# Compressing the samples' values before their keys, with the prompt's last weights kept, and a narrow weight unit laid out without holes

## The chip, the cores and the metric

The kernel runs on one core of one Trainium2 chip. The metric is the device time of one execution in microseconds. TensorE (PE) does the matrix products and has its own weight loads (PEld), VectorE (DVE), ScalarE (ACT) and GpSimd (POOL) work beside it, and SyncE (SP) issues nearly all of the transfers (DMA).

## The reference, cut to what matters

One layer of a hybrid decoder works on 512 prompt tokens and on 8 samples of 4 tokens (a model width of 1024, all in float32). A first feed-forward block (FFN1) is followed by a mixing stage, in which a state-space part and a sparse attention part share one input projection and one output projection, and then by a second feed-forward block (FFN2).

```python
def compress(k, w1, w2, pe):              # keys and values, each with weights of its own
    ch = k.reshape(bsz, n_str, CMP_STRIDE, NSA_KV_HEADS, HEAD_DIM)
    first = jnp.einsum('bnsgd,sdh->bngh', ch, w1[:CMP_STRIDE])
    second = jnp.einsum('bnsgd,sdh->bngh', ch, w1[CMP_STRIDE:])
    pre = first[:, :-1] + second[:, 1:] + jnp.einsum('sd,sdh->h', pe, w1)
    return jax.nn.gelu(pre) @ w2
...
    kc = compress(k_c, lw['cmp_k_w1'], lw['cmp_k_w2'], lw['cmp_k_pe'])
    vc = compress(v_c, lw['cmp_v_w1'], lw['cmp_v_w2'], lw['cmp_v_pe'])
```

`compress` is applied twice: to the prompt's own keys and values (512 tokens), and to the cached ones of the 8 samples (1024 tokens each, read through a page table). The order in which keys and values are compressed does not change what is computed.

## The kernel before, in words

**Products.** Every float32 operand of a large product is split into a high part and a remainder, and each block of 128 rows costs three matmuls: high by high (L319), remainder of the data by high weight (L320), high by remainder of the weight (L321). `gemm` at L312 issues them.

**Weights.** Weights come in units of 128 x 8 x 128 (512 KB), through the DMA queue of SP, into a pool of three buffers for each part (`w_hi` and `w_lo`), which are taken in turn. `Weights.get` (L174) hands out the next unit. Units that have a name were split ahead, during FFN1, by `Ahead.run` (L200), and lie in DRAM as `high_` and `rest_` arrays, so that getting one is two DMAs of 512 KB (L181). `c0` and `c1` are the two halves of the keys' compression weights, `c2` and `c3` those of the values'. `dg` is a narrow unit of 128 x 8 x 32, the weights of the gates; it lies in a 128 x 8 x 128 buffer with holes, so that each of its DMAs moves 1024 pieces of 128 bytes.

**Order.** The mixing stage is written as generators that a table interleaves. Its first phase projects (`q0`, `vw`, `kc`, `c0`, `dg`, ... in the table's order, where `c0` to `c3` there stand for prompt compression steps), the second runs attention of the prompt (steps `p`), compression of the samples (steps `k`) and more projections (`x`). The program's instructions are then ordered for each engine at build time, by a scheduler that simulates a timeline; so a small edit can move instructions of engines that it does not name.

**Compression of the prompt** (`compress_prompt`, L881): for kv = 0 (keys, `c0` and `c1`) and kv = 1 (values, `c2` and `c3`) 48 matmuls at L893, a transpose at L902, a GELU, a small product (L910 for keys, L923 for values). The keys end in `Kc`, whose remainder parts are put in place by four small DMAs (L920). `po` of L923, a tile named `tp`, reads `ge_a`, which lies in a pool that is closed at the end of the first phase; tiles of the next phase that take its place (`at_m`, `at_p`, and the pool `S.more`) wait until L923 has read it.

**Compression of the samples** (`compress_sample`, L1376): four times over, two samples' pages are loaded into `pg`; then for kv = 0 and kv = 1 the pages are split (`cs_H` on ACT at L1394; `cs_L` at L1395, the first sample's on DVE, the second's on POOL), multiplied in 48 matmuls (24 for each half unit), and finished by `cs_x` (L1402) and a GELU. In the first of the four rounds the units are got from DRAM once more: `c0` and `c1` for keys, `c2` and `c3` for values, the last of them into a buffer of `S.more`. The remainder `cs_L` of kv = 0 lies in the phase's pool `gp`, that of kv = 1 in `S.more`.

**Attention of the prompt** (`attend_prompt`, L1021): scores against the compressed keys (`sc<-Kc`, L1035), scores of a window (`sc<-K`, L1056 to L1058), their softmax (`at_m` on DVE L1065 and L1067, `at_p` on ACT L1066, then POOL L1069), transposes (L1097) and products with the values (L1087).

Of the kernel before, what the change touches and what calls it, by code (L numbers as in the profile page):

```python
# [25 lines left out]
F32 = mybir.dt.float32  # L26
# [3 lines left out]
AF = mybir.ActivationFunctionType  # L30
# [121 lines left out]
    IN_COL[f"x{_i}"] = 512 + 128 * _i  # L152


class Weights:


# [5 lines left out]

    def fetch(self, ap):

        _, nk, m = ap.shape
        raw = self.raws[0].tile([128, 8, 128], F32, name="w_raw", bufs=self.raws[1])
        self.dma.dma_start(raw[:, :nk, :m], ap)
        return raw

    def load(self):
# [2 lines left out]
    def get(self, pool=None):  # L174
        nc, ap = self.nc, self.units[self.n]
        hi, lo = ((pool or self.pool).tile([128, 8, 128], F32R, name=n, bufs=1 if pool else 3) for n in ("w_hi", "w_lo"))
        if isinstance(ap, str):
            self.n += 1
            _, nk, m = self.ahead.units[ap].shape
            for t, src in zip((hi, lo), self.ahead.parts[ap]):  # L180
                self.dma.dma_start(t.bitcast(F32)[:, :nk, :m], src[:, :nk, :m])  # L181
            return hi, lo
        if not self.raw:
            self.load()
        raw = self.raw.pop(0)
        self.n += 1
        _, nk, m = ap.shape
        nc.scalar.activation(hi[:, :nk, :m], raw[:, :nk, :m], AF.Copy)  # L188
        nc.vector.tensor_tensor(lo[:, :nk, :m], raw[:, :nk, :m], hi.bitcast(F32)[:, :nk, :m], op=OP.subtract)  # L189
        return hi, lo  # L190


class Ahead:
# [6 lines left out]
    def run(self, W, pool):  # L200
        nc, names = self.nc, list(self.units)
        raw = W.fetch(self.units[names[0]])
        yield
        for i, n in enumerate(names):
            _, nk, m = self.units[n].shape
            hi = pool.tile([128, 8, 128], F32R, name="a_hi", bufs=2)
            r, h = raw[:, :nk, :m], hi.bitcast(F32)[:, :nk, :m]
            nc.scalar.activation(hi[:, :nk, :m], r, AF.Copy)  # L208
            nc.vector.tensor_tensor(r, r, h, op=OP.subtract)  # L209
            for dst, t in zip(self.parts[n], (h, r)):  # L210
                W.dma.dma_start(dst[:, :nk, :m], t)
            if i + 1 < len(names):
                raw = W.fetch(self.units[names[i + 1]])
            yield
# [3 lines left out]
def step_kernel(ctx, tc, I, O, stop=99):  # L218
    nc = tc.nc
# [5 lines left out]
    def f32(t):  # L225
        return t.bitcast(F32)
# [5 lines left out]
    def split(hi, lo, src):  # L232
        nc.scalar.activation(hi, src, AF.Copy)  # L233
        nc.vector.tensor_tensor(lo, src, f32(hi), op=SUB)  # L234

    def pcol(k):
        a, b = P_OFF[k]
        return par[:, a:b]
# [13 lines left out]
    units = []  # L252
# [8 lines left out]
    seen = []  # L261
    named = {}

    def unit(name, ap):
        named[name] = ap
        units.append(name)

    for step in T0_ORDER + T1_ORDER + T2_ORDER:
        if step in ("c0", "c1", "c2", "c3"):
            unit(step, I["w1"][int(step[1])])  # L270
        elif step == "dg":
            unit(step, I["wdg"])
        elif step == "k" and seen.count("k") < 2:
            units.extend(f"c{seen.count('k') * 2 + i}" for i in range(2))
        elif step == "x":
            unit(f"x{seen.count('x')}", I["win"][IN_TILES.index(f"x{seen.count('x')}")])
        elif step in IN_TILES:
            unit(step, I["win"][IN_TILES.index(step)])
        seen.append(step)
# [8 lines left out]
    W = Weights(nc, wpool, units, nc.sync, ahead)  # L288
# [281 lines left out]
    def gelu2(x, pool, n):  # L570

        p = x.shape[0]
        a = pool.tile([128, n], F32, name="ge_a", bufs=1)
        nc.scalar.activation(a[:p], x, AF.Square)
        nc.vector.tensor_scalar(a[:p], a[:p], 0.044715, 1.0, op0=MUL, op1=ADD)
        nc.vector.tensor_tensor(a[:p], a[:p], x, op=MUL)
        nc.scalar.activation(a[:p], a[:p], AF.Tanh, scale=GELU_C)
        nc.vector.scalar_tensor_tensor(a[:p], a[:p], 1.0, x, op0=ADD, op1=MUL)
        return a
# [225 lines left out]
    def proj_kvq(n1, S, gp, pp):  # L805
# [6 lines left out]
        for kv in range(2):  # L812
            pe = pcol("pe")[:, kv * 16:kv * 16 + 16].rearrange("p (a s) -> p s a", a=2)
            nc.vector.tensor_copy(cT[kv][:, :, 64:66], pe)
        cmp_ = compress_prompt(S, cT, gp, pp)
        def tile_(name):
            t = IN_TILES.index(name)
# [63 lines left out]
    def compress_prompt(S, cT, gp, pp):  # L881
        w2 = pcol("w2")
        for kv in range(2):
            cH = gp.tile([128, 8, 66], F32R, name="cH")
            cL = gp.tile([128, 8, 66], F32R, name="cL")
            split(cH, cL, cT[kv])

            ps = pp.tile([128, 2, 128], F32, name="mm", bufs=2)
            for half in range(2):
                wh, wl = W.get()  # L890
                for k in range(8):
                    for x, w in ((cH, wh), (cL, wh), (cH, wl)):
                        nc.tensor.matmul(ps[:66, half], x[:, k], w[:, k], start=k == 0 and x is cH and w is wh,  # L893
                                         stop=k == 7 and w is wl)
                if half == 0:
                    yield
            fs = gp.tile([128, 8, 66], F32, name="cp_f", tag="cL").rearrange("p a b -> p (a b)")[:66, :256]
            nc.vector.tensor_copy(fs, ps[:66].rearrange("p a b -> p (a b)"))

            px = pp.tile([128, 512], F32, name="tp", bufs=2)  # L900
            for half in range(2):
                nc.tensor.matmul(px[:, :65], fs[:, half * 128:half * 128 + 128], ident[:66, half:half + 65],  # L902
                                 start=half == 0, stop=half == 1)
            nc.vector.tensor_copy(S.peb[:, kv:kv + 1], px[:, 64:65])
            x = gp.tile([128, 2, 32], F32, name="cp_x", bufs=1)
            nc.scalar.activation(x.rearrange("p g n -> p (g n)"), px[:, :64], AF.Identity, bias=S.peb[:, kv:kv + 1])
            ge = gelu2(x.rearrange("p g n -> p (g n)"), gp, 64)
            po = pp.tile([128, 512], F32, name="tp", bufs=2)
            if kv == 0:
                nc.tensor.matmul(po[0:64, :64], w2[:, 0:64], ge, start=True, stop=True)  # L910
                kc = gp.tile([128, 2, 32], F32, name="cp_kc", tag="cp_x", bufs=1).rearrange("p g n -> p (g n)")[:64]
                nc.scalar.activation(kc, po[0:64, :64], AF.Copy, scale=0.5)
                for g in range(2):
                    src = kc[:, g * 32:g * 32 + 32]
                    for dup in range(2):
                        nc.scalar.activation(S.Kc[dup * 64:dup * 64 + 64, g, 0], src, AF.Copy)
                    lo_ = gp.tile([64, 32], F32R, name="cp_lo", bufs=2)
                    nc.vector.tensor_tensor(lo_, src, f32(S.Kc)[0:64, g, 0], op=SUB)
                    for dup in range(2):
                        nc.sync.dma_start(f32(S.Kc)[dup * 64:dup * 64 + 64, g, 1], f32(lo_))  # L920
            else:
                for g in range(2):
                    nc.tensor.matmul(po[0:32, g * 64:g * 64 + 64], ge[:, g * 32:g * 32 + 32], w2[:, 64:128],  # L923
                                     start=True, stop=True)
                nc.scalar.activation(S.Vc, po[0:32, 0:128].rearrange("p (g d) -> p g d", g=2), AF.Copy, scale=0.5)
            yield
# [448 lines left out]

    def compress_sample(S, gp, pp):  # L1376
        w2 = pcol("w2")
        units = []
        for pr in range(4):
            raw = []  # L1380
            for b in range(2):
                raw.append(S.pages.tile([128, 8, 256], F32, name="pg", bufs=3))
                pages(raw[b], I["cmp"], pr * 2 + b)
            for kv in range(2):
                if pr == 0:
                    units.append([W.get(), W.get(pool=S.more if kv else None)])
                wts = units[kv]

                cH = gp.tile([128, 16, 16, 8], F32R, name="cs_H", bufs=2)
# [1 line left out]
                for b in range(2):  # L1391
                    o = (slice(None), slice(None), slice(b * 8, b * 8 + 8))
                    r = raw[b][:, :, kv * 128:kv * 128 + 128].rearrange("p i (a n) -> p a i n", n=8)
# [18 lines left out]
                dst = S.vcS[:, pr] if kv else S.kcT[:, pr * 2:pr * 2 + 2].rearrange("p b c -> p (b c)")  # L1412
# [283 lines left out]
```

## Time and profile before

| | us |
|---|---|
| median of three runs | 1272.11 |
| the three runs | 1269.2, 1272.11, 1685.08 |
| the profiled execution | 1272.05 |
| its span, from first to last instruction | 1270.3 |
| PE busy in the span | 1230.0 (97 %) |

The profiled execution is told by its span, and 1.75 us lie around it. Time stamps below are microseconds from the span's start. The mean granted clock of TensorE in the span was 0.987 of full speed. The run of 1685.08 was a disturbed one.

The mixing stage lies between 395 and 785 us; the first phase meets the second between 485 and 520 us.

### The profile page before, as it was taken

What the parts mean: (1) busy time and instruction counts of PE and PEld (TensorE: products, weight loads), DVE (VectorE), ACT (ScalarE), POOL (GpSimd) and SP (SyncE); (2) the same over time, 40 slices, a digit from 0 to 9 for tenths busy, and PEclk for the clock granted to TensorE, in tenths of its full rate; (3) what the DMA queues carried; (4) which work ended last, traced back from release to release, by engine and by line L of the source; (5) the groups of instructions that cost most, each with busy time, mean ns of one, the idle gap of its engine ahead of it and who ended that gap; (6) DMA issues with size and microseconds to landing.
All of it is one profiled execution on the core that took longest, in us unless ns stands there. A gap on an engine that the chain in (4) does not pass through costs nothing.

```text
span 1270.3 us, 24550 instructions
## 1 busy us (share of the span) xinstructions
PE 1230.0 (97%) x9810; PEld 1165.2 (92%) x9810; DVE 743.8 (59%) x1525; ACT 479.5 (38%) x913; POOL 242.3 (19%) x225
## 2 busy tenths in 40 slices
PE   7999999999999998999999999999999999999994
PEld 7999999999999997888877677899999999999994
DVE  5443443454543887766777675557666666644446
ACT  5343333443333444444544223334333333332223
POOL 0000000002232322542433543000000000035440
PEclk9999999999999998999999999899999999999997
DMA  8666665688773857443341581453222222223312
GB/s 315 201 229 207 235 216 213 226 292 273 257 237 113 261 208 260 134 137 133 105 134 35 172 322 39 160 199 96 86 84 84 86 95 86 80 76 92 92 46 71
DMA packets 89314, 202.79 MB, mean 160 GB/s; under 512 B 23160, under 2 KB 42304, under 8 KB 89200
## 3 DMA queue, kind: packets, MB, share of 16 engines
q1 hardware_dynamic: 86080, 192.56, 45.6%
q0 software_dynamic: 1968, 4.48, 1.1%
q10 hardware_dynamic: 1152, 4.19, 0.8%
q8 instruction: 77, 1.26, 0.4%
q14 instruction: 37, 0.30, 0.1%
HBM read 153.86 MB, written 46.32 MB: 158 GB/s over the span
## 4 chain that ended last, share of the span: by engine, by line
PE 91%; DMA 4%; DVE 3%; issue 1%; ACT 1%; SPq 1%; DVEq 0%; ACTq 0%; POOL 0%; POOLq 0%
PE mm L321 22%; PE mm L320 22%; PE mm L319 22%; PE pj L321 3%; PE pj L320 3%; PE pj L319 3%; PE pv L1087 3%; PE tp L1097 1%; PE acc L320 1%; PE acc L319 1%; PE acc L321 1%; DMA w_lo<-rest_c 1%; PE sc L1056 1%; PE sc L1058 1%; DMA win<-in_kwin 1%
## 5 line engine op out<-in xcount | busy, mean ns | idle before, releaser
L319 PE MATMUL mm<-XH,w_hi 128*128 128x272 f32 (+1 forms) x1408 | 407.1, 289 | 6.4 <-ACT XH L233 6.4
L320 PE MATMUL mm<-XL,w_hi 128*128 128x272 f32 (+1 forms) x1408 | 408.6, 290 | 0.3 <-DVE XL L234 0.3
L321 PE MATMUL mm<-XH,w_lo 128*128 128x272 f32 (+1 forms) x1408 | 408.2, 290 | 0.0
L319 PEld LDWEIGHTS mm<-XH,w_hi 128*128 128x128 f32 x1408 | 267.7, 190 | 6.5 <-ACT XH L233 6.4
L320 PEld LDWEIGHTS mm<-XL,w_hi 128*128 128x128 f32 x1408 | 267.2, 190 | 0.8 <-DVE XL L234 0.6
L321 PEld LDWEIGHTS mm<-XH,w_lo 128*128 128x128 f32 x1408 | 266.6, 189 | 0.1
L189 DVE TENSOR_TENSOR w_lo<-w_raw,w_hi 128x1024 fp32r<-128x1024 f32 (+1 forms) x133 | 160.9, 1210 | 112.9 <-ACT w_hi L188 111.6
L321 PE MATMUL mm<-hH,w_lo 128*128 128x272 f32 x704 | 203.9, 290 | 0.0
L320 PE MATMUL mm<-hL,w_hi 128*128 128x272 f32 x704 | 203.4, 289 | 0.0
L319 PE MATMUL mm<-hH,w_hi 128*128 128x272 f32 x704 | 203.0, 288 | 0.0
L188 ACT ACTIVATE w_hi<-w_raw 128x1024 fp32r<-128x1024 f32 (+1 forms) x133 | 137.2, 1032 | 155.3 <-PE mm L320 142.7
L328 POOL TENSOR_TENSOR res<-XH,XL 128x544 f32<-128x544 f32 x16 | 21.7, 1360 | 627.6 <-DVE hL L234 594.3
L320 PEld LDWEIGHTS mm<-hL,w_hi 128*128 128x128 f32 x704 | 132.6, 188 | 0.2
L319 PEld LDWEIGHTS mm<-hH,w_hi 128*128 128x128 f32 x704 | 132.5, 188 | 0.1
L321 PEld LDWEIGHTS mm<-hH,w_lo 128*128 128x128 f32 x704 | 132.3, 188 | 0.2
L209 DVE TENSOR_TENSOR w_raw<-w_raw,a_hi 128x1024 f32<-128x1024 f32 (+1 forms) x36 | 43.3, 1203 | 113.6 <-ACT a_hi L208 113.6
L319 PE MATMUL pj<-XH,w_hi 128*128 128x274 f32 (+3 forms) x336 | 98.8, 294 | 1.1 <-DMA w_hi<-high_dg 1.1
L320 PE MATMUL pj<-XL,w_hi 128*128 128x274 f32 (+3 forms) x336 | 99.1, 295 | 0.0
L321 PE MATMUL pj<-XH,w_lo 128*128 128x272 f32 (+3 forms) x336 | 98.6, 294 | 0.1
L233 ACT ACTIVATE hH<-hf 128x272 fp32r<-128x272 f32 x88 | 37.6, 428 | 131.0 <-DVE hf L488 99.0
L208 ACT ACTIVATE a_hi<-w_raw 128x1024 fp32r<-128x1024 f32 (+1 forms) x36 | 37.5, 1042 | 83.8 <-DMA w_raw<-in_win 49.9
L321 PEld LDWEIGHTS pj<-XH,w_lo 128*128 128x128 f32 (+1 forms) x336 | 62.2, 185 | 4.2 <-issue 3.1
(461 smaller groups left out, 2058.5 us busy)
## 6 DMA issues: line engine op xcount, KB each, us to landing
w_raw<-in_wg SPq DMA_DIRECT2D x44, 512.0 KB, 3.7
w_raw<-in_wu SPq DMA_DIRECT2D x44, 512.0 KB, 3.6
w_raw<-in_wd SPq DMA_DIRECT2D x32, 512.0 KB, 3.9
w_raw<-in_win SPq DMA_DIRECT2D x20, 512.0 KB, 4.3
pg<-in_cmp SPq DMA_DIRECT2D x64, 128.0 KB, 2.7
w_raw<-in_wd SPq DMA_DIRECT2D x16, 384.0 KB, 3.2
w_raw<-in_wout SPq DMA_DIRECT2D x8, 512.0 KB, 4.6
high_o<-a_hi SPq DMA_DIRECT2D x8, 512.0 KB, 3.6
```

The source lines that it names most:

```text
L188: nc.scalar.activation(hi[:, :nk, :m], raw[:, :nk, :m], AF.Copy)
L189: nc.vector.tensor_tensor(lo[:, :nk, :m], raw[:, :nk, :m], hi.bitcast(F32)[:, :nk, :m], op=OP.subtract)
L208: nc.scalar.activation(hi[:, :nk, :m], r, AF.Copy)
L209: nc.vector.tensor_tensor(r, r, h, op=OP.subtract)
L233: nc.scalar.activation(hi, src, AF.Copy)
L319: nc.tensor.matmul(ps, hi[:, k, :m], rh(k0 + k), start=b, stop=False)
L320: nc.tensor.matmul(ps, hi[:, k, :m], rl(k0 + k), start=False, stop=False)
L321: nc.tensor.matmul(ps, lo[:, k, :m], rh(k0 + k), start=False, stop=e)
L328: nc.gpsimd.tensor_tensor(out, a, b, op=ADD)
L1056: nc.tensor.matmul(s, q, S.K[:, br, h // 4, 0, :w], start=True, stop=False)
L1058: nc.tensor.matmul(s, q, S.K[:, br, h // 4, 1, :w], start=False, stop=True)
L1087: nc.tensor.matmul(pv[hh * 64:hh * 64 + 64, hp % 2], v, t[:, hh], start=start, stop=stop)
```

## The change

Two things change. First, `packed` views a tile as if it held only the unit's own columns, so that the narrow unit `dg` lies as 128 rows of 1 KB, in the raw buffer, in DRAM and in the weight buffers; units of 512 KB read the same. Second, `compress_prompt` keeps the buffers of its last two units (`c2` and `c3`, those of the values) in `S.cw`; `compress_sample` takes kv = 1 first, with these, and gets only `c0` and `c1` once more (the latter now into `S.more`). The list of units loses `c2` and `c3` for the samples.

```diff
+def packed(t, shape):
+    _, nk, m = shape
+    return t.rearrange("p k m -> p (k m)")[:, :nk * m].rearrange("p (k m) -> p k m", k=nk)
...
-        self.dma.dma_start(raw[:, :nk, :m], ap)
+        self.dma.dma_start(packed(raw, ap.shape), ap)
...
+            hi, lo = (packed(t, shape) for t in (hi, lo))
             for t, src in zip((hi, lo), self.ahead.parts[ap]):
-                self.dma.dma_start(t.bitcast(F32)[:, :nk, :m], src[:, :nk, :m])
+                self.dma.dma_start(t.bitcast(F32), packed(src, shape))
...
             for dst, t in zip(self.parts[n], (h, r)):
-                W.dma.dma_start(dst[:, :nk, :m], t)
+                W.dma.dma_start(packed(dst, shape), t)
...
-        elif step == "k" and seen.count("k") < 2:
-            units.extend(f"c{seen.count('k') * 2 + i}" for i in range(2))
+        elif step == "k" and seen.count("k") == 1:
+            units.extend(("c0", "c1"))
...
             ps = pp.tile([128, 2, 128], F32, name="mm", bufs=2)
+            S.cw = []
             for half in range(2):
                 wh, wl = W.get()
+                S.cw.append((wh, wl))
...
-        units = []
+        units = {1: S.cw}
...
-            for kv in range(2):
-                if pr == 0:
-                    units.append([W.get(), W.get(pool=S.more if kv else None)])
+            for kv in (1, 0):
+                if kv not in units:
+                    units[kv] = [W.get(), W.get(pool=S.more)]
```

SP, where the first phase meets the second: the loads of the samples' weights and the remainder of the prompt's compressed keys. Before:

```order
L181 DMA w_hi_5830<-high_c0_73 128x1024
L181 DMA w_lo_5831<-rest_c0_74 128x1024
L181 DMA w_hi_5834<-high_c1_89 128x1024
L181 DMA w_lo_5835<-rest_c1_90 128x1024
L181 DMA w_hi_6139<-high_c2_93 128x1024
L181 DMA w_lo_6140<-rest_c2_94 128x1024
L920 DMA Kc_4650<-cp_lo_5603 64x32 x2
L920 DMA Kc_4650<-cp_lo_5609 64x32 x2
L181 DMA w_hi_6143<-high_c3_95 128x1024
L181 DMA w_lo_6144<-rest_c3_96 128x1024
```

And now:

```order
L186 DMA w_hi_6131<-high_c0_73 128x1024
L186 DMA w_lo_6132<-rest_c0_74 128x1024
L927 DMA Kc_4650<-cp_lo_5603 64x32 x2
L927 DMA Kc_4650<-cp_lo_5609 64x32 x2
L186 DMA w_hi_6135<-high_c1_89 128x1024
L186 DMA w_lo_6136<-rest_c1_90 128x1024
```

`c0` still comes first, the small DMAs into `Kc` move ahead of all but `c0`, `c1` takes the place of `c3` behind them, and four DMAs of 512 KB are gone.

PE, a little later: the last of `c0`'s 24 matmuls, and what stands around the values' last product of the prompt (`tp<-par,ge_a`). Before:

```order
L321 MATMUL mm_5844<-cs_H_5838,w_lo_5831 128x256
L319 MATMUL mm_5844<-cs_H_5838,w_hi_5834 128x256
L320 MATMUL mm_5844<-cs_L_5839,w_hi_5834 128x256
L923 MATMUL tp_5767<-par_61,ge_a_5761 32x64 x2
L321 MATMUL mm_5844<-cs_H_5838,w_lo_5835 128x256
```

And now:

```order
L1042 MATMUL sc_5898<-Kc_4650,QS_4638 128x64 x4
L324 MATMUL mm_6145<-cs_H_6139,w_hi_6131 128x256
L930 MATMUL tp_5767<-par_61,ge_a_5761 32x64 x2
L325 MATMUL mm_6145<-cs_L_6140,w_hi_6131 128x256
L326 MATMUL mm_6145<-cs_H_6139,w_lo_6132 128x256
L1063 MATMUL sc_5956<-K_4649,QS_4638 128x128
L1064 LDWEIGHTS idb_4655
L1064 MATMUL sc_5956<-mk_d_4654,idb_4655 128x128
L1065 MATMUL sc_5956<-K_4649,QS_4638 128x128
```

Before, 22 more matmuls of `c1` follow the product, then the first of `c2`, the scores against `Kc` and the next window scores. Now the scores against `Kc` stand ahead of it, two matmuls of `c0` behind it, and then three sets of window scores (`sc_5956`, whose buffer `at_p` of the set before must have read, `sc_5970` and `sc_5996`). Behind these stand the other 47 matmuls of the values' unit (its first stands further up, ahead of this excerpt), and then the 24 of `c1`.

DVE at the same place: the end of the prompt's GELU, and the first work of the second phase. Before:

```order
L578 SCALAR_TENSOR_TENSOR ge_a_5761<-ge_a_5761,cp_x_5759 128x64
L1065 TENSOR_REDUCE at_m_5939<-sc_5935 128x1
L1065 TENSOR_REDUCE at_m_5953<-sc_5949 128x1
L1395 TENSOR_TENSOR cs_L_6148<-pg_5778,cs_H_6147 128x16x64
L1067 RECIPROCAL at_m_5939<-at_m_5939 128x1
```

And now:

```order
L583 SCALAR_TENSOR_TENSOR ge_a_5761<-ge_a_5761,cp_x_5759 128x64
L1403 TENSOR_TENSOR cs_L_5831<-pg_5778,cs_H_5830 128x16x64
L1072 TENSOR_REDUCE at_m_5931<-sc_5927 128x1
L1072 TENSOR_REDUCE at_m_5945<-sc_5941 128x1
L1046 TENSOR_TENSOR ac_p_5909<-sc_5898,ac_p_5909 128x256
```

The remainder of the values' pages stood behind the two maxima of the softmax, and stands ahead of them now.

## Rows read from the trace of the kernel before

**Rows 1.** The page's first part: busy time, share, instructions.

```profile
PE 1230.0 (97%) x9810; PEld 1165.2 (92%) x9810; DVE 743.8 (59%) x1525; ACT 479.5 (38%) x913; POOL 242.3 (19%) x225
```

**Rows 2.** Waits of PE, 395 to 530 us: total, times, longest.

```profile
PE mm L319 <- DMA w_hi<-high_c: 2.4, 1, 2.4
...
PE pj L319 <- DMA w_hi<-high_dg: 1.1, 1, 1.1
```

**Rows 3.** Stretches of the span, with columns as its first line says.

```profile
core 0: us, PE busy (x) PEld busy (x) DVE busy (x) ACT busy (x) POOL busy (x), PEclk, DMA share, GB/s
490.00:500.00 10.00, 5.79 (x44) 5.25 (x45) 5.99 (x13) 5.08 (x16) 1.54 (x1) 0.79 1.03 342
500.00:510.00 10.00, 10.00 (x77) 9.77 (x76) 6.30 (x13) 3.85 (x13) 4.24 (x3) 0.87 0.50 169
510.00:520.00 10.00, 7.95 (x66) 6.92 (x65) 6.99 (x20) 5.13 (x11) 6.26 (x5) 1.00 0.61 174
```

**Rows 4.** Timeline of SP's queue: start, us, line, transfer issued.

```profile
488.88 0.86 SPq L181 DMA_DIRECT2D w_hi<-high_c  x1
...
492.81 0.40 SPq L181 DMA_DIRECT2D w_lo<-rest_c  x1
493.31 4.91 SPq L920 DMA_DIRECT2D Kc<-cp_lo  x4
503.63 0.33 SPq L181 DMA_DIRECT2D w_hi<-high_c  x1
```

**Rows 5.** Transfers issued at 492.81 and at 493.31: KB, us to landing.

```profile
w_lo<-rest_c SPq DMA_DIRECT2D x1, 512.0 KB, 10.1
Kc<-cp_lo SPq DMA_DIRECT2D x1, 8.0 KB, 9.7
```

**Rows 6.** Timeline of PE: start, us, [idle before, what ended it].

```profile
496.52 0.58 PE L319 MATMUL mm<-cs_H,w_hi 128*128 128x256 f32 x1 [2.42 <-DMA w_hi<-high_c]
...
502.00 0.41 PE L319 MATMUL mm<-cs_H,w_hi 128*128 128x256 f32 x1
...
502.95 0.41 PE L923 MATMUL tp<-par,ge_a 128*32 128x64 f32 x4
...
503.63 0.28 PE L320 MATMUL mm<-cs_L,w_hi 128*128 128x256 f32 x1
503.75 0.28 PE L321 MATMUL mm<-cs_H,w_lo 128*128 128x256 f32 x1
...
506.15 0.97 PE L1035 MATMUL sc<-Kc,QS 128*128 128x64 f32 x8
...
514.04 0.28 PE L321 MATMUL mm<-cs_H,w_lo 128*128 128x256 f32 x1
```

**Rows 7.** Timeline of DVE, in the same columns.

```profile
503.70 0.49 DVE L1065 TENSOR_REDUCE at_m<-sc 128x1 f32<-128x128 f32 x2 [6.22 <-DMA Kc<-cp_lo]
504.10 3.27 DVE L1395 TENSOR_TENSOR cs_L<-pg,cs_H 128x1024 fp32r<-128x1024 f32 x1
...
529.33 1.23 DVE L1395 TENSOR_TENSOR cs_L<-pg,cs_H 128x1024 fp32r<-128x1024 f32 x1
```

**Rows 8.** Timeline of POOL.

```profile
503.90 2.39 POOL L1395 TENSOR_TENSOR cs_L<-pg,cs_H 128x1024 fp32r<-128x1024 f32 x1 [12.26 <-DMA Kc<-cp_lo]
...
529.51 3.29 POOL L1395 TENSOR_TENSOR cs_L<-pg,cs_H 128x1024 fp32r<-128x1024 f32 x1 [3.96 <-ACT cs_H L1394]
```

**Rows 9.** Timeline of ACT.

```profile
504.15 0.37 ACT L1066 ACTIVATE at_p<-sc,at_m 128x128 f32<-128x128 f32 x1 [0.48 <-DVE at_m L1065]
...
515.47 0.46 ACT L1402 ACTIVATE cs_x<-mm,peb 128x256 f32<-128x256 f32 x1
515.82 1.99 ACT L1394 ACTIVATE cs_H<-pg 128x1024 fp32r<-128x1024 f32 x2
```

**Rows 10.** Two stretches of one us, in the columns of rows 3.

```profile
659.00:660.00 1.00, 0.00 (x0) 0.00 (x0) 0.00 (x0) 0.65 (x2) 0.00 (x0) 1.00 1.08 389
690.00:691.00 1.00, 0.94 (x12) 0.94 (x13) 0.81 (x3) 0.24 (x1) 0.00 (x0) 0.66 0.00 0
```

**Rows 11.** Timeline of PE at these two stretches.

```profile
660.08 0.63 PE L1097 MATMUL tp<-ident,at_p 128*128 128x128 f32 x4 [1.66 <-ACT pT L1098]
...
690.06 1.76 PE L1087 MATMUL pv<-pT,V 128*64 128x128 f32 x14 [2.09 <-DVE pT L1098]
```

**Rows 12.** Transfers issued at 427.05 and at 428.52: KB, us to landing.

```profile
w_hi<-high_dg SPq DMA_DIRECT2D x1, 128.0 KB, 3.8
...
pg<-in_cmp SPq DMA_DIRECT2D x1, 128.0 KB, 3.4
```

More of the change, by code (lines that the diff above doesn't have):

```diff
@@ L164, in fetch @@
     def fetch(self, ap):
-        _, nk, m = ap.shape
         raw = self.raws[0].tile([128, 8, 128], F32, name="w_raw", bufs=self.raws[1])
-        self.dma.dma_start(raw[:, :nk, :m], ap)
+        self.dma.dma_start(packed(raw, ap.shape), ap)
         return raw
@@ L178, in get @@
             self.n += 1
-            _, nk, m = self.ahead.units[ap].shape
+            shape = self.ahead.units[ap].shape
+            hi, lo = (packed(t, shape) for t in (hi, lo))
             for t, src in zip((hi, lo), self.ahead.parts[ap]):
-                self.dma.dma_start(t.bitcast(F32)[:, :nk, :m], src[:, :nk, :m])
+                self.dma.dma_start(t.bitcast(F32), packed(src, shape))
             return hi, lo
@@ L204, in run @@
         for i, n in enumerate(names):
-            _, nk, m = self.units[n].shape
+            shape = self.units[n].shape
             hi = pool.tile([128, 8, 128], F32R, name="a_hi", bufs=2)
-            r, h = raw[:, :nk, :m], hi.bitcast(F32)[:, :nk, :m]
-            nc.scalar.activation(hi[:, :nk, :m], r, AF.Copy)
+            r, h = packed(raw, shape), packed(hi, shape).bitcast(F32)
+            nc.scalar.activation(packed(hi, shape), r, AF.Copy)
             nc.vector.tensor_tensor(r, r, h, op=OP.subtract)
             for dst, t in zip(self.parts[n], (h, r)):
-                W.dma.dma_start(dst[:, :nk, :m], t)
+                W.dma.dma_start(packed(dst, shape), t)
             if i + 1 < len(names):
```

## The prediction

> **What bounds the kernel now.** I read the page's first part before anything else: PE is busy for 1230.0 us, 97 % of the span [rows 1], and no other engine comes near. So only what PE has to do, what it waits for and the clock it is granted can move the end; a transfer or another engine counts where PE waits for it, and only there. The second view was PE's waits inside the stretch that the change edits. Two of them name transfers that the change touches: 2.4 us for the samples' first unit and 1.1 us for `dg` [rows 2]. [...] Everything below happens between 488 and 520 us. After 520 the kernel goes on as before, with PE always busy, so a delay that PE has there reaches the end in full.
>
> **The transfers: nothing.** Four DMAs of 512 KB go. DMA share is 1.03 from 490 to 500 [rows 3], so the queue is full, and it is tempting to hand the 2.42 us that PE waits for `c0` [rows 6] to the change. But `c0` is issued first, at 488.88, and the removed ones after it, up to 492.81 [rows 4]. That last one lands 10.1 us later, at 502.9; the 8 KB issued into `Kc` behind it lands 9.7 us later, at 503.0 [rows 5]. A transfer of 8 KB that takes as long as the 512 KB ahead of it has queued behind it: this queue serves in order. So `c0` lands when it did, and PE's wait for it stays, with the low clock that follows it. What does come sooner is `Kc`, by up to the 5 us of the four transfers ahead of it. Does somebody wait for that? DVE's row at 503.70 and POOL's at 503.90 name `Kc` as the releaser, after 6.22 and 12.26 us [rows 7, 8]. That is the trap of the profile: these tiles take the place of a pool that the prompt's last product (L923) still reads, that product runs from 502.95 to 503.36 [rows 6], and 0.34 us after it DVE starts. Both came within half a microsecond, and only one moves. Taken at 0; the bounds are 0 and the wait of 2.42 with the low clock behind it, priced in the rivals.
>
> **`dg`: -0.4.** Its load of 128 KB in pieces of 128 bytes takes 3.8 us from issue to landing, and the same 128 KB in rows of 1 KB, issued 1.5 us later in the same queue, 3.4 [rows 12]. The difference comes off a wait of 1.1 [rows 2]; bounds 0 and -1.1. The other transfers of this unit (its fetch and two writes in FFN1) lie beside a busy PE and are taken at nothing; were that cover gone, each could cost a fraction of the same 0.4.
>
> **The order: +1.9.** This is what the diff doesn't show. I walk PE, DVE, ACT and POOL through the new order with durations from the rows.
> - Before, PE had 24 matmuls of `c0` and two of `c1`, then L923 at 502.95. Now 22 of `c0` (the 22nd starts at 502.00) and the eight scores against `Kc`, 0.97 [rows 6], then that product: it ends at about 503.6 instead of 503.36.
> - Before, PE then had 22 matmuls of `c1`, 0.12 apart (503.63 to 503.75, rows 6), to cover the softmax. Now two, so PE is through by 503.85, and next are window scores that wait for `at_p` of the set before.
> - DVE wakes at 503.95 and now does `cs_L` first, 1.23 when it goes ahead of POOL [rows 7]: 505.2. Then come `at_m` and `at_p`; before, `at_p` ended 0.82 after `at_m` began (503.70, 504.15 and 0.37, rows 7, 9). So PE goes on at about 506.1: **a new idle stretch of 2.2 us**.
> - Three sets of window scores take 0.9. Next are the values' 47 matmuls, which read POOL's half of `cs_L`. POOL starts 0.2 behind DVE, as it did (503.90 behind 503.70), and takes 3.29 when DVE went first [rows 8]: 507.45, another 0.4 idle.
> - 71 matmuls at 0.12 and two more sets of scores (0.6) bring PE to 516.6; before it had done the same work at 514.16 [rows 6].
> - Now the next unit's data. Values end at 513.1; then ACT needs 0.46 for `cs_x` and 1.99 for two `cs_H` [rows 9], and POOL 2.39 [rows 8]: 518.0. PE, through with `c1` at 516.6, idles 1.4. Before, it idled 10 - 7.95 = 2.05 [rows 3], all of it between 514.2 and 518.05, so at 518.05 it had done 3.9 - 2.05 = 1.85 of work beyond that point. **PE is 1.9 behind**, and stays so. From the second round of pages on the two orders alternate the units in the same manner.
>
> DVE ahead of POOL is where I chose. The nearest row for the other case is the one at 504.10, where POOL had begun 0.20 earlier and DVE took 3.27 in place of 1.23 [rows 7, 8]. [...]
>
> **The clock: +2.0.** The new idle stretch has a price of its own. An idle stretch of 2.09 us ended at 690.06, and the granted clock of the microsecond behind it is 0.66; one of 1.66 ended at 660.08, and the clock just ahead of its end is 1.00 [rows 10, 11]. 2.2 us is nearest to the first. Bounds: 0, and what a fallen clock cost from 496.52 on, at most 3.2: the `c0` matmuls took until about 502.6, 6.1 us, where 24 at 0.12 take 2.9 (a short wait for the unit's second half is in the 6.1). I take 2.0, since part of such a low stretch would pass while PE waits for POOL.
>
> **Sum.** The profiled execution took 1272.05 us (span 1270.3 and 1.75 around it), 0.06 under the median of 1272.11, so no correction is needed. 1272.05 + 0 - 0.4 + 1.9 + 2.0 = **1275.5**. A difference under about 2 % (25 us) is no more than a measurement of this kernel can tell from no change; all my cases lie inside it.
>
> **Rivals.**
> - *The clock holds.* The same walk without the 2.0: 1273.5. For it: 2.2 us is just over 2.09, and a walk of eight steps may be wrong by half a microsecond. Against: nothing makes the stretch shorter, unless `Kc` frees DVE earlier after all.
> - *POOL first.* Both wake on the same event; if POOL takes `cs_L` first, DVE's part ends 3.3 to 3.4 us after it, `at_p` at 508.1, and PE starts 47 matmuls at 509.1 instead of 507.45. That is 1.65 more: 1277.2. For it: the order of starts at 503.90 and 504.10. Against: before, DVE had two `at_m` to do first.
> - *Not a queue in order* (the other side). If the 16 engines share themselves among the transfers in flight, `c0` gains from the 2 MB that are gone: its wait of 2.42 and up to 3.2 of low clock vanish, and the walk starts earlier but idles as much: 1275.5 - 5.6 = 1269.9, and without a second fall of the clock 1267.9. It decides from the point at which `c0` lands before 494.1, when PE is ready. Against it: the 8 KB that took 9.7.
> - *The wait recurs* (clearly slower). In each later round POOL's `cs_L` comes at the end of 0.46 + 1.99 + 2.39 = 4.8 us, against 48 matmuls at 0.12 (5.8) that cover it. With POOL at its slow 3.29 it is 5.7. If attention steps no longer stand between, or POOL is held longer than 3.4, idle stretches of 1.4 with a fallen clock (2.0) come in three more rounds: 1275.5 + 3 x 3.4 = 1285.7. Against: the order before has the same chain there, and PE was busy.
> - *The change does nothing here.* If another order covers the softmax by luck of timing, only `dg` is left: 1271.7.
>
> **Chances.** Forecast 0.40; clock holds 0.18; POOL first 0.15; not in order 0.08; recurs 0.07; nothing 0.07; 0.05 for what I did not see. The range 1269 to 1281 leaves out the recurring wait, half of the case that is not in order, and the unseen: 0.16, and a little of the forecast's own edges. Faster by over 2 %: 0.01. Slower by over 2 %: 0.03. Within: 0.96.
>
> **What would show it.** In the profile of the changed kernel: PE's wait for `w_hi<-high_c` still near 2.4, and the clock of 490 to 500 still near 0.8; `Kc` landing by 499 and yet DVE starting `cs_L` only after the product of L930; PE idle for about 2 us near 504, put down to ACT's `at_p`, and again for POOL's `cs_L` near 507; the clock of 505 to 515 well below 1; `w_hi<-high_dg` at about 0.7. I am wrong if the first wait is gone, or if PE has no idle time between 503 and 508.

## The result, and the profile after

| | kernel before | changed kernel |
|---|---|---|
| median of 20 runs, us | 1270.78 | 1280.03 |
| span of the profiled execution, us | 1270.3 | 1279.5 |
| mean granted clock | 0.987 | 0.985 |

The ratio of the changed kernel to the one before is 1.0074, with a 95 % interval of 1.0059 to 1.0089: 7.5 to 11.3 us slower, where +3.5 was forecast. The time lies inside the range of 1269 to 1281. The sum of 1275.5 is 4.5 us under it, and the change itself, about 9.4 us, is some 6 us larger than forecast: the median of 20 runs of the kernel before is 1.3 us under the time on which the sum was built. The prediction took a difference under 2 % for one that can't be told from none; with 20 runs of each, the interval is 0.3 % wide, and a change of 0.7 % is told.

Where the time goes is read off four matmuls that both kernels have. The first fence is the kernel before: start, us and idle time of PE's first prompt matmul of the values, its last matmul of the samples' compression, one near the end of the mixing stage and one near the end.

```profile
485.45 0.22 PE L893 MATMUL mm<-w_hi,cH 128*66 128x128 f32 x1
...
589.43 0.28 PE L321 MATMUL mm<-cs_H,w_lo 128*128 128x256 f32 x1
...
796.23 1.19 PE L1294 MATMUL sc<-bx,xt_s 32*128 32x512 f32 x1 [1.55 <-DVE bx L1291]
...
1253.63 0.73 PE L404 MATMUL ln_ps<-res,ones 128*128 128x272 f32 x2 [0.72 <-DVE res L371]
```

The same four of the changed kernel, whose lines are numbered 5 to 7 higher:

```profile
486.47 0.22 PE L900 MATMUL mm<-w_hi,cH 128*66 128x128 f32 x1
...
597.79 0.28 PE L326 MATMUL mm<-cs_H,w_lo 128*128 128x256 f32 x1
...
804.38 1.19 PE L1301 MATMUL sc<-bx,xt_s 32*128 32x512 f32 x1 [1.55 <-DVE bx L1298]
...
1263.12 0.72 PE L409 MATMUL ln_ps<-res,ones 128*128 128x272 f32 x2 [0.72 <-DVE res L376]
```

The changed kernel is 1.0 us behind at the first, 8.4 at the second, 8.15 at the third and 9.5 at the last. So 7.4 of the 9.5 arise in the hundred microseconds in which the samples are compressed. These are differences of one trace each, and the kernel's undisturbed runs lie up to 18 us apart, so a part of one or two microseconds is not sure. The changed kernel's stretches there, in the columns of rows 3, answer to those rows; the last one is where the next surprise lies:

```profile
490.00:500.00 10.00, 7.24 (x52) 6.57 (x53) 6.57 (x14) 5.09 (x16) 1.54 (x1) 0.83 0.53 160
500.00:510.00 10.00, 8.43 (x49) 8.00 (x48) 5.61 (x21) 2.58 (x11) 5.79 (x6) 0.67 0.66 220
510.00:520.00 10.00, 8.59 (x72) 8.39 (x71) 5.82 (x7) 5.10 (x7) 3.27 (x2) 0.99 0.33 97
...
545.00:560.00 15.00, 11.67 (x78) 9.34 (x77) 11.24 (x32) 8.34 (x25) 6.52 (x7) 0.89 0.29 117
```

The kernel before, in that last stretch, had no idle time and a clock of 1.00:

```profile
545.00:560.00 15.00, 15.00 (x114) 12.64 (x114) 11.61 (x31) 9.08 (x23) 5.19 (x7) 1.00 0.40 146
```

From 490 to 500 PE is busier than before (7.24 against 5.79). From 500 to 510 it is idle and slow, as forecast. But from 545 to 560 it loses another 15 - 11.67 = 3.3 us of idle time and 15 x 0.11 = 1.7 of clock, 5.0 together, of which the prediction has nothing. Idle time and lost clock add up here, since the clock fell after the idle time had ended: PE's rows below have the wait end at 553.66, and the granted clock is 1.00 until 554.6 and 0.50 from 555 to 558. Lost clock is an estimate throughout: a stretch times what its granted clock lacks of 1.00. In this trace the matmuls of one unit started 0.21 us apart at the clock of 0.50 (from 556.09 on) and 0.12 apart at 1.00 (from 558.15 on).

### The profile page after: what moved, and what is told of

The parts are those of the page before. It is cut to its first block, busy times and chain, and to the rows that moved or that the text cites. A ratio compares the mean times of both kernels' runs of the same rounds, so it can differ in the third digit from the quotient of the medians.

```text
span 1279.5 us, 24536 instructions
## 1 busy us (share of the span) xinstructions
PE 1238.6 (97%) x9810; PEld 1170.4 (91%) x9810; DVE 742.7 (58%) x1525; ACT 480.2 (38%) x913; POOL 243.2 (19%) x225
## 5 line engine op out<-in xcount | busy, mean ns | idle before, releaser
L324 PE MATMUL pj<-XH,w_hi 128*128 128x272 f32 (+3 forms) x336 | 99.3, 296 | 1.0 <-DMA w_hi<-high_dg 1.0
L325 PE MATMUL pj<-XL,w_hi 128*128 128x272 f32 (+3 forms) x336 | 98.9, 295 | 0.0
L324 PEld LDWEIGHTS pj<-XH,w_hi 128*128 128x128 f32 (+1 forms) x336 | 62.6, 186 | 3.5 <-DVE vcat L853 1.2
```

Source lines behind the costliest of these rows:

```text
L324: nc.tensor.matmul(ps, hi[:, k, :m], rh(k0 + k), start=b, stop=False)
L325: nc.tensor.matmul(ps, hi[:, k, :m], rl(k0 + k), start=False, stop=False)
```

## The experiments

Each ratio is against runs of the kernel before on the same chip. The theory of the first set: the order of the units costs, since the values' `cs_L` lies where it can only be written after the prompt's last product.

**1. The layout of `dg` alone.** The kernel before with `packed`; `compress_prompt` and `compress_sample` as they were.

> Only the narrow unit dg is laid out without holes; the samples' compression is as before. Theory (the order of keys and values is what costs): within 1.5 us of the kernel before (ratio 0.999 to 1.001), PE's wait for w_hi<-high_dg between 0.6 and 1.1 us. Rival 1 (the lag of 1.0 us that the changed kernel already has at 482 us comes from dg, and grows later): slower by 1 to 3 us, with a new short wait near 438. Rival 2 (the other transfers matter): same as the theory.

Measured: 1269.98 us, ratio 1.0006 (0.9987 to 1.0025). The layout does nothing that can be measured. PE's wait for `dg` was 1.5, above the 0.6 to 1.1 expected.

**2. The rest alone**: the change without `packed`.

> Values first with the prompt's last weights kept; dg with holes as before. Theory: all of the slowdown is here, 8 to 11 us over the kernel before, with PE idle 1.3 to 2.2 near 504 for at_p, 1.4 near 518 for cs_L, and 2.5 to 3.2 near 553 for ge_a, the clock at half after the first and the last of them. Rival 1 (dg): 5 to 8 us. Rival 2: same as the theory.

Measured: 1281.63 us, ratio 1.0091 (1.0062 to 1.0120). All of the slowdown is here, and PE's waits are the expected ones (the first line is two waits, and the longer is the one near 553):

```profile
PE tp L1413 <- DVE ge_a L578: 3.5, 2, 2.9
PE mm L320 <- POOL cs_L L1397: 1.4, 1, 1.4
PE sc L1058 <- ACT at_p L1068: 1.3, 1, 1.3
```

**3. The pools of `cs_L` exchanged.**

```diff
-                cL = (S.more if kv else gp).tile([128, 16, 16, 8], F32R, name="cs_L", bufs=1)
+                cL = (gp if kv else S.more).tile([128, 16, 16, 8], F32R, name="cs_L", bufs=1)
```

> The changed kernel with the two pools of cs_L exchanged: the values' remainder, now needed first, lies in gp and the keys' in S.more. Theory (values first costs because the first unit's cs_L lies where it can only be written after the prompt's last product): the values' 48 matmuls now run at 492 to 499 us, where PE waited for c0, no idle over 1 us between 493 and 508 and no fall of the clock there; 4 to 9 us faster than the changed kernel at least, near or under the kernel before (1264 to 1272). Rival 2 (the kept weights and the moved transfers cost, not the order): no faster than the changed kernel by more than 2 us.

Measured: 1270.64 us, ratio 0.9999 (0.9979 to 1.0020). The slowdown is gone, with the transfers and the kept weights of the change left in. But the gain over the kernel before did not come: PE ran the values' matmuls early, and then had nothing left to cover the softmax.

```profile
506.23 0.46 PE L1063 MATMUL sc<-K,QS 128*128 128x128 f32 x1 [3.76 <-ACT at_p L1073]
```

DVE and POOL in the same run show why `at_p` was so late:

```profile
503.06 2.42 DVE L580 TENSOR_SCALAR ge_a<-ge_a 128x256 f32<-128x256 f32 x1
505.41 0.48 DVE L1072 TENSOR_REDUCE at_m<-sc 128x1 f32<-128x128 f32 x2
```

```profile
502.60 2.73 POOL L1403 TENSOR_TENSOR cs_L<-pg,cs_H 128x1024 fp32r<-128x1024 f32 x1 [10.82 <-PE tp L930]
```

A GELU step that takes 0.28 at 551.74 in the changed kernel took 2.42 and ended at 505.48, as POOL's `cs_L` ended at 505.33, and `at_m` stood behind it. From 545 to 560, where the changed kernel lost 5.0 us, this one had no idle time and a clock of 1.00, which the theory had not foreseen.

**4. Values first, with their weights read again**: the units' list is `c2`, `c3`, `c0`, `c1`, and `kv` goes (1, 0); nothing is kept.

> Values first, but c2 and c3 are got from DRAM once more, so that all eight DMAs are there; cs_L as in the changed kernel; dg packed. Theory (order): as slow as the changed kernel or slower, 1278 to 1284, since PE again finds no unit whose cs_L can be written before the prompt's last product but the keys', whose weights come third now. Rival 2 (kept weights and moved transfers cost): back to the kernel before, 1270 to 1274.

Measured: 1282.75 us, ratio 1.0089 (1.0062 to 1.0116). With the order of the change and all eight DMAs back, the kernel is as slow. This run also has waits that the changed kernel lacks, 1.18 and 2.26 for `w_hi` of the samples' units and 1.99 for the prompt's product, so by itself it does not show that the order alone costs as much. With run 3, which keeps the weights and lacks the transfers and is not slow, it does rule out that these two are the cause.

**5. One half of `cs_L` moved from POOL to DVE in the changed kernel**: the one that POOL holds from 547.96 to 551.17.

```diff
-                    (nc.gpsimd if b else nc.vector).tensor_tensor(cL[o], r, f32(cH)[o], op=SUB)
+                    (nc.gpsimd if b and (pr, kv) != (3, 1) else nc.vector).tensor_tensor(cL[o], r, f32(cH)[o], op=SUB)
```

> The changed kernel, with the one cs_L half that POOL holds from 547.96 for 3.2 us (the last round's values) done on DVE; PE's, ACT's and SP's orders are the same as in the changed kernel. Theory (DVE's GELU and softmax stand still while POOL runs cs_L, and PE's wait of 2.9 us for ge_a at 553.7 and the fallen clock behind it come of that): the wait shrinks to 1.0 to 1.8 us, the clock does not fall there, 2 to 4 us faster than the changed kernel. Rival (the wait comes of the order in which DVE takes ge_a behind four softmax steps, whoever does cs_L): the wait stays at 2.5 or more, same time, since DVE has 1.2 us more to do.

Measured: 1280.51 us, ratio 1.0082 (1.0056 to 1.0108): no faster than the changed kernel. PE's order is the same as there, and the wait did shrink by half:

```profile
551.42 1.11 PE L1419 MATMUL tp<-par,ge_a 128*128 128x64 f32 x4 [1.44 <-DVE ge_a L583]
```

but the clock, which was to hold, averaged 0.77 in place of 0.89, and the stretch lost as much as before (1.65 idle and 15 x 0.23 = 3.5 of clock):

```profile
545.00:560.00 15.00, 13.35 (x80) 10.44 (x79) 10.17 (x34) 8.40 (x25) 3.60 (x6) 0.77 0.25 102
```

**6 to 8. All of `cs_L` on DVE** (`nc.vector` in that line for both halves): with the exchanged pools, in the changed kernel, and in the kernel before.

> The changed kernel with the pools of cs_L exchanged, as in the run before, and all cs_L on DVE. Theory: the row of 2.42 us for a GELU step of 0.28 at 503.06 is DVE standing still behind POOL; without it at_m comes 2.2 us earlier, PE's wait at 506.2 falls from 3.8 to 1.0 to 1.8 us, the clock holds, and the kernel is 3 to 5 us faster than with the exchanged pools alone (1265 to 1268). Rival (DVE gets 8 x 1.23 us more on the same path, and becomes what PE waits for): the same or slower, 1270 to 1276.

> The changed kernel with all cs_L on DVE. Theory: 3 to 7 us faster than the changed kernel (1273 to 1277), since both the late cs_L at 507 and 518 and the late ge_a at 553 go; what is left is the wait behind the prompt's last product, 1.5 to 2.5 us near 504 with the fallen clock. Rival (order of the units alone): no faster than the changed kernel by over 2 us.

> The kernel before with all cs_L on DVE. Theory: PE's waits there (0.9, 0.5 and 0.6 us between 515 and 518) get shorter; otherwise its order had covered the stalls: 0 to 2 us faster than the kernel before. Rival: if the stalls cost the kernel before as much as the changed one, 3 to 6 us faster.

Measured: 1269.90 us, ratio 0.9989 (0.9969 to 1.0009); 1280.70 us, 1.0061 (1.0030 to 1.0091); 1275.48 us, 1.0029 (1.0012 to 1.0046). All three expectations missed. In the first, PE's one wait of 3.76 became two, 1.63 for `at_p` and 1.20 for `cs_L`, which DVE now did alone. The third is the telling one: the old order too became slower, and by a wait for `ge_a` near 549, which it had never had.

```profile
PE tp L1409 <- DVE ge_a L578: 2.6, 1, 2.6
```

So a wait for `ge_a` came (2.60) with no `cs_L` on POOL at all. In the changed kernel the `cs_L` on POOL is still about half of it: run 5 took that one away, and 2.91 became 1.44.

**9 to 11. The table of the second phase begins with p, then k** (it was k, then p), so that DVE takes `at_m` ahead of `cs_L`: with the exchanged pools, in the changed kernel, in the kernel before.

```diff
-T1_ORDER = "k p p p k k p p p k p k k p k p k p k p p x r x x a p p x p x p x a".split()
+T1_ORDER = "p k p p k k p p p k p k k p k p k p k p p x r x x a p p x p x p x a".split()
```

> The changed kernel with the pools of cs_L exchanged and with the second phase's table beginning with p and then k, in place of k and then p, so that DVE takes at_m ahead of cs_L and of the GELU step that stood still behind POOL. Theory (PE's wait behind the prompt's last product is set by where at_m stands on DVE): the wait of 3.8 us at 506 falls to 0.3 to 1.0, no fall of the clock there, 590 us is reached 3 to 6 us earlier than by the kernel before, and the whole is faster than both kernels, 1264 to 1268. Rival (DVE's work is only pushed behind, and PE waits as long for cs_L of the keys): same as with the exchanged pools alone, 1269 to 1272.

> The changed kernel with the table beginning with p and then k: DVE takes at_m ahead of cs_L, as in the kernel before; the values' cs_L still lies in S.more. Theory: the wait for at_p near 504 shrinks from 1.6 to under 0.8 us, but PE then finds only the values' unit, whose cs_L ends 3 to 3.5 us after the prompt's last product, and waits 1 to 2.5 us for that: 0 to 3 us faster than the changed kernel. Rival (the place of at_m on DVE was the whole of the cost): 7 to 10 us faster, level with the kernel before.

> The kernel before with the table beginning with p and then k; DVE had at_m first already. Theory: within 2 us of the kernel before, since nothing ahead of PE moves. Rival (the start with p is better for its own reasons): 3 us faster or more.

Measured: 1278.52 us, ratio 1.0074 (1.0051 to 1.0098); 1277.93 us, 1.0055 (1.0030 to 1.0079); 1270.65 us, 1.0009 (0.9987 to 1.0031). The first was to be the best kernel of all, and is as slow as the changed one. Its wait near 503 was 1.8 us, and a stretch that the exchanged pools had passed without loss now has the `ge_a` wait:

```profile
543.48 0.40 PE L1417 MATMUL tp<-ge_a,par 128*64 128x128 f32 x4
...
548.09 0.73 PE L1419 MATMUL tp<-par,ge_a 128*128 128x64 f32 x4 [2.68 <-DVE ge_a L583]
```

The second is the reverse: no loss from 545 to 560 (PE busy throughout, clock 1.00), but the clock averaged 0.59 and 0.50 in the twenty microseconds from 490, so that a kernel without the wait for `ge_a` is slow all the same.

```profile
490.00:500.00 10.00, 8.27 (x51) 7.82 (x52) 5.68 (x13) 4.77 (x16) 1.33 (x1) 0.59 0.48 138
500.00:510.00 10.00, 8.07 (x38) 7.22 (x37) 6.47 (x20) 2.57 (x11) 4.16 (x5) 0.50 0.46 157
```

**What separates the kernels with the wait from those without** is how much work PE has between two products behind GELUs: the last one of the first round and the first one of the second round. `gelu2` has one buffer, `ge_a`, so the second GELU can't begin before PE has read the first. From each trace, in us: where the two products start, the time between these starts less the wait, and the wait.

| kernel | the two products | between them, less the wait | wait for the second |
|---|---|---|---|
| before | 543.24, 547.99 | 4.75 | none |
| 1 | 542.92, 547.67 | 4.75 | none |
| 11 | 542.99, 547.69 | 4.70 | none |
| 3 (pools exchanged) | 541.57, 546.26 | 4.69 | none |
| 6 (pools exchanged, all on DVE) | 539.44, 544.21 | 4.77 | none |
| 10 | 543.58, 549.85 | 6.27 | none |
| changed | 547.67, 553.66 | 3.08 | 2.91 |
| 2 | 549.23, 555.21 | 3.08 | 2.90 |
| 5 | 546.91, 551.42 | 3.07 | 1.44 |
| 4 | 551.07, 554.98 | 2.75 | 1.16 |
| 7 | 552.20, 557.77 | 3.65 | 1.92 |
| 8 (kernel before, all on DVE) | 544.36, 548.88 | 1.92 | 2.60 |
| 9 | 543.48, 548.09 | 1.93 | 2.68 |

With 4.7 us or more between them there is no wait, with 3.7 or less there is one. How long it is does not follow from this distance: 3.08 goes with 2.91, and 2.75 with 1.16. A second buffer for `ge_a`, the direct test of the single one, was not tried.

**12. That distance, by one step of the table.** One step of the changed kernel's table moves; PE's order is untouched up to the first of the two products, and the second goes from 13 to 30 rows behind it. Behind that, PE's order differs from the changed kernel's for some 40 us, so it is not the distance alone that moves.

```diff
-T1_ORDER = "k p p p k k p p p k p k k ...
+T1_ORDER = "k p p p k p k p p k p k k ...
```

> The changed kernel with one step of the second phase's table moved: the third k (the second round's values) comes one p later. PE's order is the same up to the first round's last product (row 4144); the second round's first product moves from 13 to 30 rows behind it. Theory (ge_a has one buffer, so the GELU of the second round's values can start only when PE has read the first round's keys, and the chain ACT, DVE, ACT, DVE of about 5 us is covered by 30 rows of PE and not by 13): no wait of PE for ge_a between 545 and 560 us and no fall of the clock there; junction as in the changed kernel (wait for at_p near 504, clock at half); 3 to 6 us faster than the changed kernel, 1274 to 1277. Rival (DVE is late in this stretch whatever PE's order): the wait moves with the product and stays at 2 us or more; same time, 1279 to 1282.

Measured: 1276.61 us, ratio 1.0049 (1.0029 to 1.0068), 3.4 us under the changed kernel and in the range expected, though the two intervals overlap. PE's waits from 484 to 600 us, longest first:

```profile
PE sc L1063 <- ACT at_p L1073: 1.6, 1, 1.6
PE mm L324 <- DMA w_hi<-high_c: 1.5, 1, 1.5
PE mm L900 <- DMA w_lo<-rest_c: 1.4, 1, 1.4
PE pv L1094 <- DVE tc L1090: 1.4, 1, 1.4
PE mm L325 <- POOL cs_L L1403: 1.4, 1, 1.4
```

Of the waits for `ge_a` only one of 0.65 at 522.10 is left, which the changed kernel has too; the one near 553 is gone, PE's waits at the junction for `at_p` and `cs_L` are as they were, and so far the theory holds. The other half fails: a wait of 1.4 for `tc`, at 551.7, took part of its place, and the clock fell there all the same.

```profile
545.00:560.00 15.00, 13.40 (x85) 10.10 (x84) 12.34 (x41) 8.92 (x29) 7.58 (x9) 0.80 0.25 100
```

Idle time is 1.6 us here and lost clock 15 x 0.20 = 3.0, 4.6 together where the changed kernel lost 5.0. So moving the products apart removes this wait, but hardly the loss of the stretch, and where the 3.4 us were gained was not worked out.

None of the versions beats the kernel before by more than its interval; number 6 comes nearest.

## Why the prediction was right, and where it fell short

**The transfers: taken at 0; the wait was 1.7 us shorter, and whether the transfers did that is open.** In the changed kernel `c0`, issued at 489.50, landed in 5.7 us (transfers issued around then: KB, us to landing):

```profile
w_hi<-high_c SPq DMA_DIRECT2D x1, 512.0 KB, 5.7
```

PE waited 0.76 for it, in place of 2.42 [rows 6]:

```profile
495.35 0.36 PE L324 MATMUL mm<-cs_H,w_hi 128*128 128x256 f32 x1 [0.76 <-DMA w_hi<-high_c]
...
501.51 0.41 PE L930 MATMUL tp<-par,ge_a 128*32 128x64 f32 x4
503.94 0.47 PE L1063 MATMUL sc<-K,QS 128*128 128x128 f32 x1 [1.57 <-ACT at_p L1073]
...
518.53 0.38 PE L325 MATMUL mm<-cs_L,w_hi 128*128 128x256 f32 x1 [1.41 <-POOL cs_L L1403]
```

This wait scatters from trace to trace as much as that. Runs 8 and 11 have all the transfers of the kernel before behind `c0`, run 12 has those of the changed kernel; one row of each, in this order:

```profile
496.14 0.58 PE L319 MATMUL mm<-cs_H,w_hi 128*128 128x256 f32 x1 [0.85 <-DMA w_hi<-high_c]
495.65 0.58 PE L319 MATMUL mm<-cs_H,w_hi 128*128 128x256 f32 x1 [1.50 <-DMA w_hi<-high_c]
494.56 0.35 PE L324 MATMUL mm<-cs_H,w_hi 128*128 128x256 f32 x1 [1.52 <-DMA w_hi<-high_c]
```

From the issue of `c0` to the end of PE's wait it took 7.6, 6.8 and 6.6 us with the other transfers (before, 8, 11) and 5.9, 5.9, 6.5, 6.6 and 6.8 without (changed, 2, 10, 12, 7). In the kernel before, the next four landed one after the other in order of issue, at 499.0, 500.3, 501.6 and 502.9, as the prediction had it. So a gain of up to 1.7 us is possible and not shown, and a fallen clock remained behind the wait in either kernel (0.50 from 497 to 500 in the changed one, from 496 to 502 before). In run 4 PE waited 2.26 for `w_hi` at 501.41, and the time was 2.7 us longer than the changed kernel's, with intervals that overlap: this term decided little.

**`dg`: -0.4.** Too small to be seen: run 1 gives nothing outside -1.7 to +3.2 us. PE's wait for it was 1.0 in the changed kernel and 1.5 in run 1, where it was 1.1 [rows 2], so no gain shows.

**The order at the junction: +1.9 and +2.0, right in mechanism and near in size.** The prompt's product came at 501.5, 1.4 us before that of rows 6. DVE took `cs_L` first, and POOL's half, begun 0.10 us later, took 3.33 where 3.29 was taken:

```profile
501.96 1.23 DVE L1403 TENSOR_TENSOR cs_L<-pg,cs_H 128x1024 fp32r<-128x1024 f32 x1 [3.88 <-PE tp L930]
503.11 0.48 DVE L1072 TENSOR_REDUCE at_m<-sc 128x1 f32<-128x128 f32 x2
```

```profile
502.06 3.33 POOL L1403 TENSOR_TENSOR cs_L<-pg,cs_H 128x1024 fp32r<-128x1024 f32 x1 [9.80 <-PE tp L930]
```

PE's new wait was 1.57, where 2.2 was worked out, the clock fell (0.67 from 500 to 510), and the wait for the next round's `cs_L` was 1.41, where 1.4 was worked out. From 500 to 520, idle time and lost clock are 2.98 and 3.4 us, against 2.05 and 1.3 [rows 3]: 3.0 more, where the two terms sum to 3.9. With PE's shorter wait for `c0` ahead of it, the junction came out nearly even: from 484 to 520 the changed kernel lost 11.7 us to idle time and clock and the kernel before 11.4, 0.3 apart, where the sum had 3.9. So what the sum priced is not what made the kernel slower. That the time lies inside the range is luck: a loss from 545 to 560 that the sum did not hold stands in place of the one that it did.

**"From the second round on the two orders alternate the units in the same manner": this is the step that failed,** and with it "After 520 the kernel goes on as before, with PE always busy". Most of the loss, 5.0 of the 7.4 us, is between 545 and 560. The two products that have 4.75 us of PE's work between them before have 3.08 now. Before, on PE:

```profile
543.24 0.66 PE L1411 MATMUL tp<-par,ge_a 128*128 128x64 f32 x4
...
547.99 0.44 PE L1409 MATMUL tp<-ge_a,par 128*64 128x128 f32 x4
```

In the changed kernel, on PE, and then ACT and DVE between the two:

```profile
547.67 0.44 PE L1417 MATMUL tp<-ge_a,par 128*64 128x128 f32 x4
...
553.66 0.66 PE L1419 MATMUL tp<-par,ge_a 128*128 128x64 f32 x4 [2.91 <-DVE ge_a L583]
```

```profile
549.13 0.43 ACT L579 ACTIVATE ge_a<-cs_x 128x256 f32<-128x256 f32 x1
552.64 0.42 ACT L582 ACTIVATE ge_a<-ge_a 128x256 f32<-128x256 f32 x1 [3.08 <-DVE ge_a L581]
```

```profile
549.06 2.13 DVE L1075 TENSOR_TENSOR at_m<-at_m,G 128x1 f32<-128x1 f32 x1
...
551.74 0.28 DVE L580 TENSOR_SCALAR ge_a<-ge_a 128x256 f32<-128x256 f32 x1
...
553.20 0.41 DVE L583 SCALAR_TENSOR_TENSOR ge_a<-ge_a,cs_x 128x256 f32<-128x256 f32 x1
```

The GELU has five steps. The first, on ACT, starts once the earlier product has been read and ACT has done what is queued ahead. The second waits on DVE behind a softmax step of one column that took 2.13 us beside POOL's `cs_L`, for 0.16 at 551.29; the third is DVE's as well, the fourth (L582) is on ACT, and the last (L583) on DVE: 6.0 us from product to product, with 3 us of PE's work between them. I had the rival of a recurring wait, with a chance of 0.07, and tied it to POOL's `cs_L` and the next unit's matmuls; it came by `ge_a`, with 0.66 us at 522.80 and 2.91 at 553.66. I had read the two orders around the junction and not, row by row, where the second round begins.

**What stays open.** Of the 7.4 us, 0.3 are the junction from 484 to 520, 0.7 a wait for `ge_a` at 522.8, 5.0 this stretch; the other 1.4 were not placed, and one trace of each kernel does not resolve them. The table and run 12 show what makes the wait for `ge_a`; that the loss of the stretch goes with it is not shown, since there a wait for `tc` and a fallen clock cost about as much. Why the clock falls in one kernel and holds in the next with much the same waits was not worked out. The last 1.35 us, from 804 to 1263, go with a longer stretch at a clock of 0.50 behind the third matmul (from 804 to 814, against 797 to 802 in the kernel before; mean clock 0.75 in the 20 us from 804, against 0.83 in those from 796), for which no run has a cause.

## What to carry to other kernels

Where a build-time scheduler orders the instructions, compare the two orders along the whole stage, and look for pairs that share one buffer: how far apart they stand on the waiting engine, in microseconds of its work, against the chain that has to fit between. A wait at the head of a queue is worth less than it looks when what it covers must then be covered otherwise: run 3 took away the wait for `c0`, and a wait of 3.76 for the softmax took its place. Half a wait may be worth nothing: in run 5 it fell from 2.91 to 1.44 us, the mean clock of the stretch fell from 0.89 to 0.77, and the time stayed the same. And a wait read off one trace is to be looked up in several before a cause is given for it: the wait for `c0` was 0.85, 1.50 and 2.42 in three kernels with the same transfers.

## What the runs showed of the hardware

- Some DVE instructions took longer while POOL ran `cs_L`, down to an operation on one column: `at_m<-at_m,G` 2.13 us at 549.06 and 1.10 at 504.31, for 0.16 at 551.29 (changed kernel), and a GELU step 2.42 at 503.06 (run 3), for 0.28. They ended 0.02, 0.02 and 0.15 us behind POOL's `cs_L`, at 551.19, 505.41 and 505.48. Others kept their time: in the changed kernel's POOL stretch from 502.06 to 505.39 two `at_m<-sc` at 503.11 took 0.48, as two did at 505.41 in run 3, with POOL's `cs_L` over.

```profile
504.31 1.10 DVE L1075 TENSOR_TENSOR at_m<-at_m,G 128x1 f32<-128x1 f32 x1
```

- In two pairs of `cs_L` halves that overlapped, the one begun first kept its time and the other took longer: in the changed kernel DVE's from 501.96 took 1.23 and POOL's from 502.06 took 3.33; in the kernel before POOL's was first [rows 7, 8]. What holds the later one up is not shown.
- From 545 to 560 the mean granted clock was 0.77 in run 5, with a wait of 1.44 us, and 0.89 in the changed kernel, with one of 2.91 and PE's order the same (one trace of each).
- In the kernel before, the four transfers of 512 KB issued on SP's queue behind the two of `c0` landed in the order of their issue, about 1.3 us apart (499.0, 500.3, 501.6 and 502.9). Whether they slow `c0` is open: from its issue to the end of PE's wait it took 6.6 to 7.6 us with them (before, 8, 11) and 5.9 to 6.8 without (changed, 2, 7, 10, 12).
